# Reversing the column order of the gate, up and down products in a four-layer hybrid encoder

## The chip, the cores and the metric

The kernel runs on one core of a Trainium2 chip, as one program. The metric is the device time of one execution in microseconds. All tensors are float32 in memory; the large products use float32r operands, that is, float32 words that TensorE takes in one pass.

## What is computed

The reference is an encoder trunk on one sequence of 256 positions and 1024 channels, four layers deep. Each layer is a token mixer (in turn RWKV-7 time mixing, stick-breaking attention, sparse attention, RWKV-7 again) and then a feed-forward block:

```
x = x + mixer(rms_norm(x, norm_mix[i]))
x = x + swiglu(rms_norm(x, norm_ffn[i]), ffn_w_gu[i], ffn_w_down[i])

def swiglu(h, w_gu, w_down):
    g, u = jnp.split(h @ w_gu, 2, axis=-1)
    return (jax.nn.silu(g) * u) @ w_down
```

`w_gu` is 1024 x 5632 (gate and up, 2816 columns each) and `w_down` is 2816 x 1024, for each of four layers.

## The kernel before

**Layout.** Activations are kept transposed: a channel block of 128 is the partition dimension and the 256 positions lie along the free dimension. Every value that goes into a large product is kept as two float32r halves, a high one and a low one (the rest), side by side: `xg[:, c]` is one channel block with 2 x 256 columns, high half first. Weights arrive in pieces of 128 x 1024 floats and are split in the same way, by a cast on ScalarE (`wh`) and a subtraction on VectorE (`wl`); half of the gate and up pieces go to a buffer called `wring` instead.

**The gate, up and query/key products** come from `gemm1` (line 908). For each of 8 channel blocks it issues two matmuls into one PSUM bank. The first has the high weights as the stationary operand and the whole 512 columns of `xg[:, c]` (both halves) as the moving one, and writes all 512 columns of the bank. The second has the low weights and the 256 columns of the high half, and adds into the first 256 columns of the bank. The feed-forward block calls it 22 times for gate and 22 times for up in each of four layers; stick-breaking attention (layer 1) calls it 16 times more for `qk`. When a bank is complete, `add2` adds its two halves to each other, on ScalarE and VectorE.

**The down products** are the loop in `ffn` (line 1052): 8 output blocks in each layer, each the sum over 22 blocks of `h`, with the same two matmuls for each block and the same widths, into a bank called `dn`.

In this document *a pair* is such a 512-column matmul and the 256-column matmul behind it. There are 4 x 44 x 8 = 1408 pairs for gate and up, 4 x 8 x 22 = 704 for down, and 16 x 8 = 128 for `qk`: 2240 pairs, 4480 matmuls.

**Order.** Nothing is issued directly. Every operation is recorded (`Plan.record`, line 334), and a list scheduler with its own table of costs puts the operations of all engines in order before any is emitted (line 779 is the one line at which nearly all are emitted, so the profile shows L779 nearly everywhere and tiles tell the operations apart). A pair is one unit for the scheduler. Costs and dependences are taken from the number of elements and from the set of columns that a view touches, whatever their order.

**Other products.** The mixers have float32r products of their own (`po`, `rp`, `kp`, `vps`, `qi` and the `qk` of the sparse layer, in `gemm2`, `out_half` and `v_gemm`), plain float32 products (`qrot`, `qss`, `kss`, `vp`, ...) and many narrow ones. `warm_o` is a dummy bfloat16 product.

Of the kernel before, what the change touches and what calls it, by code (L numbers as in the profile page):

```python
# [23 lines left out]
S = 256  # L24
D = 1024
NC = D // P
NF = 11
# [268 lines left out]
class Plan:  # L296
# [15 lines left out]
    def unit(self, at_once=1, ns=0.0):  # L312

        plan = self

        class Unit:
            def __enter__(self):
                plan.unit_op = Op("tensor")
                plan.unit_op.ns = ns

            def __exit__(self, *_):
                op, plan.unit_op = plan.unit_op, None
                op.cost /= at_once
                op.cost = op.ns or op.cost
                plan._add(op)

        return Unit()
# [63 lines left out]
    def after(self, op, preds):  # L391
        op.preds |= set(preds)
# [390 lines left out]
def trunk(ctx: ExitStack, tc: tile.TileContext, xT_in, vecs_in, wts, lora_in, consts_in, id32_in, outT, order, layers=None):  # L783
# [7 lines left out]
    pe, dve, act, pool, sp = (plan.queue(n) for n in ("tensor", "vector", "scalar", "gpsimd", "sync"))  # L791
# [3 lines left out]
    def T(shape, group=None, name="t", dtype=F32):  # L795
        return plan.tile(sb, [P] + list(shape), dtype, group, name)
# [7 lines left out]
    def bank(name, group="ps"):  # L804
        return plan.tile(psum, [P, 512], F32, group, name, "psum")
# [48 lines left out]
    def f(ap):  # L854
        return ap.bitcast(F32)


    def piece(key, raw=None, parts=None):

        i = len(order)  # L860
        order.append(key)
        r = T([PIECE], "raw", f"raw{i}") if raw is None else raw
        sp.dma_start(r, wts[i])
        h, l = (T([PIECE], "wh", f"wh{i}", F32R), T([PIECE], "wl", f"wl{i}", F32R)) if parts is None else parts
        anye.copy(h, r)
        dve.tensor_tensor(l, r, f(h), op=ALU.subtract)
        return h, l
# [26 lines left out]
    def v3(t, n):  # L894
        return t.rearrange("p (k m) -> p k m", k=n)
# [4 lines left out]
    def flat(t):  # L900
        return t.rearrange("p a b -> p (a b)")

    def add2(t, o, eng=anye):

        eng.copy(t, o[:, S:])
        dve.tensor_tensor(t, o[:, :S], t, op=ALU.add)

    def gemm1(key, x, name, group="g", raw=None, parts=None):


        out = bank(name, group)
        wh, wl = [v3(t, NC) for t in piece(key, raw, parts)]
        for c in range(NC):
            with unit():
                pe.matmul(out, wh[:, c], flat(x[:, c]), start=(c == 0), stop=False)
                pe.matmul(out[:, :S], wl[:, c], x[:, c, 0], start=False, stop=(c == NC - 1))
        return out

    def gemm2(key, xs, name):
# [76 lines left out]
    def rstd_bcast(summed=False):  # L996
        if summed:
            ss = nstate["ss"]
        else:
            ss, sq = bank("ss"), t1("ssq")  # L1000
            anye.tensor_tensor(sq, nstate["acc"][:, 0], nstate["acc"][:, 1], op=ALU.add)
            exact(ss[:, :S], onesr, sq, [T([S], "t", "ssr", F32R) for _ in range(2)])
        return rsqrt_of(ss[:, :S], S, "rstd", 1.0 / D, eps_rms)
# [15 lines left out]
    def ffn(layer, after):  # L1019
        x = nstate["xg"]  # L1020
        rsb = None
        hs = [v.rearrange("p (i k a s) -> p i k a s", i=n, k=2, a=2)
              for v, n in ((T([4096], g, "h", F32R), 4) for g in ("SA", "SZ", "PR"))]

        ring = T([6, PIECE], "QC", "wring", F32R)

        def place(n):

            return {"parts": (ring[:, n // 2 % 3], ring[:, 3 + n // 2 % 3]) if n % 2 else None}

        for i in range(NF):
            gus = T([2, 2, S], f"s{6 + i % 2}", "gus")
            gs, us = gus[:, 0], gus[:, 1]
            since = len(plan.ops)
            for k in range(2):
                add2(gs[:, k], gemm1(("g", layer, 2 * i + k), x, "gate", **place(4 * i + k)), act if i >= 0 else anye)
            if i == 0:
                rsb = rstd_bcast()[:, None, :].to_broadcast([P, 2, S])
            dve.tensor_tensor(gs, gs, rsb, op=ALU.mult)
            act.activation(gs, gs, AF.Silu)  # L1040
            for k in range(2):
                add2(us[:, k], gemm1(("u", layer, 2 * i + k), x, "up", "ps", **place(4 * i + 2 + k)), act if i >= 0 else anye)
            if i >= 1:
                plan.in_turn(since, "gate", "up")
            dve.tensor_tensor(us, us, rsb, op=ALU.mult)
            dve.tensor_tensor(us, us, gs, op=ALU.mult)
            h = hs[i // 4][:, i % 4]
            act.copy(h[:, :, 0], us)
            dve.tensor_tensor(h[:, :, 1], us, f(h[:, :, 0]), op=ALU.subtract)

        n, since = 0, len(plan.ops)
        for m in range(NC):
            o = bank("dn", "g" if m % 2 else "ps")
            for k in range(2 * NF):
                if n % NC == 0:
                    wh, wl = [v3(t, NC) for t in piece(("d", layer, n // NC))]
                h = hs[k // 8][:, k // 2 % 4, k % 2]
                with unit():
                    pe.matmul(o, wh[:, n % NC], flat(h), start=(k == 0), stop=False)
                    pe.matmul(o[:, :S], wl[:, n % NC], h[:, 0], start=False, stop=(k == 2 * NF - 1))  # L1060
                n += 1
            for a in range(2):
                dve.tensor_tensor(xt[m // 2][:, m % 2], xt[m // 2][:, m % 2], o[:, a * S:(a + 1) * S], op=ALU.add)
            if m == NC - 1:
                plan.in_turn(since, "dn")
            if m % 2:
                after(m // 2)
# [500 lines left out]
    def stick(layer, after):  # L1568
# [12 lines left out]
        for p in range(8):  # L1581
            q, k = qk_[:, p, 0], qk_[:, p, 1]
            add2(q, gemm1(("sq", p), x, "qk"))
            add2(k, gemm1(("sk", p), x, "qk"))
            if p == 0:
# [377 lines left out]
```

## Time and profile before

| | |
|---|---|
| Median of 3 runs | 1396.13 us (1396.02 to 1396.16) |
| The profiled execution, its own time | 1397.01 us |
| Its span in the trace | 1395.1 us |
| TensorE (PE) busy | 1376.2 us, 99% of the span, 10404 matmuls |
| Weight loads (PEld) busy | 1184.4 us, 85% |
| VectorE (DVE) busy | 1076.0 us, 77% |
| ScalarE (ACT) busy | 802.8 us, 58% |
| HBM traffic | 217.14 MB read, 156 GB/s over the span |
| Granted TensorE clock | 1.00 throughout |

The profile is one execution. A row of its groups gives the engine, the operation, the tile written and the tiles read, the shape, the count, then the busy time and the mean duration in nanoseconds. Matmuls overlap each other, and their ends are modelled: the duration of one says more than the time it takes from its neighbours. What one matmul costs in a dense stretch is the distance from start to start, which the chain of waits gives as a total for a run of equal matmuls. The time of an execution is its span and a little around it, here 1.9 us.

### The profile page before, as it was taken

Reading aid. Unit: us, or ns where it says so; the run is one execution under the profiler, and the core shown is the slowest. Engines: PE = TensorE matmul, PEld = TensorE weight load, DVE = VectorE, ACT = ScalarE, POOL = GpSimd, SP = SyncE. Lnnn points to the kernel's source line nnn. Section 1 sums busy time; section 2 is a strip of 40 time slices with the busy share of each in tenths; the row PEclk is TensorE's granted clock in tenths of the full one; section 3 lists DMA queues with packets and bytes.
Section 4 is the critical chain, followed back from the end, with each engine's and each line's share of the span. In section 5 each row is a group of like instructions: output and inputs, shape, how many; then the busy total and the mean of one; then the engine's idle time right before and its main releaser. Section 6 shows DMA issues by size and latency. Waiting matters only on the chain.

```text
span 1395.1 us, 25701 instructions
## 1 busy us (share of the span) xinstructions
PE 1376.2 (99%) x10404; PEld 1184.4 (85%) x10404; DVE 1076.0 (77%) x1791; ACT 802.8 (58%) x1362; POOL 7.6 (1%) x16
## 2 busy tenths in 40 slices
PE   9999999999999999999999999999999999999998
PEld 6887888888888888888988788888878877888887
DVE  7998498876676788876668988876579985888754
ACT  3765576654456676554545876654438465766532
POOL 0000000000000000000000000000000000000000
PEclk9999999999999999999999999999999999999999
DMA  6423056665654357646654336766635220567654
GB/s 225 145 91 122 19 168 205 204 178 164 191 168 150 107 180 214 203 145 194 195 167 132 95 107 212 219 190 209 187 91 170 91 92 18 168 203 209 176 172 128
DMA packets 61317, 219.84 MB, mean 158 GB/s; under 512 B 6800, under 2 KB 8080, under 8 KB 60944
## 3 DMA queue, kind: packets, MB, share of 16 engines
q1 hardware_dynamic: 61200, 218.22, 50.8%
q8 instruction: 81, 1.33, 0.4%
q14 instruction: 36, 0.29, 0.1%
HBM read 217.14 MB, written 1.05 MB: 156 GB/s over the span
## 4 chain that ended last, share of the span: by engine, by line
PE 79%; DVE 12%; DMA 4%; ACT 3%; issue 2%; DVEq 0%; ACTq 0%
PE dn L779 17%; PE up L779 14%; PE gate L779 14%; PE qk L779 6%; DMA raw<-in_wts_dram 4%; PE rp L779 3%; PE kp L779 3%; PE po L779 3%; PE vps L779 3%; PE z L779 2%; DVE wl L779 2%; DVE inv L779 2%; DVE xtmp L779 1%; PE sc L779 1%; PE attn_o L779 1%
## 5 line engine op out<-in xcount | busy, mean ns | idle before, releaser
L779 DVE TENSOR_TENSOR wl<-raw,wh 128x1024 fp32r<-128x1024 f32 x285 | 347.9, 1223 | 142.0 <-ACT wh L779 140.2
L779 ACT CAST wh<-raw 128x1024 fp32r<-128x1024 f32 x268 | 280.8, 1049 | 234.0 <-PE dn L779 99.7
L779 PE MATMUL dn<-h,wh 128*128 128x512 f32 x704 | 244.2, 390 | 0.0
L779 PE MATMUL dn<-h,wl 128*128 128x256 f32 x704 | 198.5, 282 | 0.0
L779 PEld LDWEIGHTS dn<-h,wh 128*128 128x128 f32 x704 | 132.2, 188 | 27.7
L779 PE MATMUL gate<-xg,wring 128*128 128x512 f32 x704 | 133.0, 337 | 4.0 <-DVE wring L779 3.1
L779 PEld LDWEIGHTS dn<-h,wl 128*128 128x128 f32 x704 | 133.0, 189 | 0.0
L779 PE MATMUL up<-xg,wring 128*128 128x512 f32 x704 | 132.4, 336 | 0.0
L779 PEld LDWEIGHTS gate<-xg,wring 128*128 128x128 f32 x704 | 107.4, 188 | 22.0 <-DVE wring L779 5.4
L779 PE MATMUL gate<-xg,wh 128*128 128x512 f32 x352 | 125.5, 395 | 0.2
L779 PE MATMUL up<-xg,wh 128*128 128x512 f32 x352 | 125.1, 392 | 0.0
L779 DVE TENSOR_TENSOR wring<-raw,wring 128x1024 fp32r<-128x1024 f32 x88 | 107.4, 1221 | 17.3 <-ACT wring L779 16.4
L779 PEld LDWEIGHTS up<-xg,wring 128*128 128x128 f32 x704 | 107.4, 188 | 14.4
L779 ACT CAST wring<-raw 128x1024 fp32r<-128x1024 f32 x87 | 91.5, 1052 | 33.8 <-DMA raw<-in_wts_dram 25.8
L779 PE MATMUL up<-xg,wl 128*128 128x256 f32 x352 | 98.5, 280 | 0.0
L779 PE MATMUL gate<-xg,wl 128*128 128x256 f32 x352 | 98.4, 280 | 0.0
L779 PE MATMUL qk<-xg,wh 128*128 128x256 f32 (+1 forms) x384 | 96.7, 332 | 0.0
L779 PEld LDWEIGHTS gate<-xg,wh 128*128 128x128 f32 x352 | 66.0, 188 | 16.6 <-DVE xg L779 1.3
L779 PEld LDWEIGHTS up<-xg,wh 128*128 128x128 f32 x352 | 66.1, 188 | 14.5
L779 PEld LDWEIGHTS qk<-xg,wh 128*128 128x128 f32 x384 | 64.0, 188 | 9.7 <-issue 4.2
L779 PE MATMUL qk<-xg,wl 128*128 128x256 f32 x256 | 71.7, 280 | 0.0
L779 PEld LDWEIGHTS up<-xg,wl 128*128 128x128 f32 x352 | 66.1, 188 | 0.2
(306 smaller groups left out, 2592.9 us busy)
## 6 DMA issues: line engine op xcount, KB each, us to landing
raw<-in_wts_dram SPq DMA_DIRECT2D x397, 512.0 KB, 3.7
lora<-in_lora_dram SPq DMA_DIRECT2D x2, 1536.0 KB, 9.9
xt<-in_xT_dram SPq DMA_DIRECT2D x4, 256.0 KB, 3.7
lora<-in_lora_dram SPq DMA_DIRECT2D x2, 512.0 KB, 6.1
lg<-in_lora_dram SPq DMA_DIRECT2D x8, 128.0 KB, 3.9
inv<-in_id_dram SPq DMA_DIRECT2D x2, 512.0 KB, 3.7
out_dram<-xt SPq DMA_DIRECT2D x4, 256.0 KB, 3.6
lg<-in_lora_dram SPq DMA_DIRECT2D x2, 256.0 KB, 3.6
```

The source lines that it names most:

```text
L779: getattr(getattr(nc, o.eng), method)(*map(real, args), **{k: real(a) for k, a in kw.items()})
```

## The change

Both matmuls of a pair read their moving operand with a step of -1, from the last column to the first, and write their PSUM columns with a step of -1 too. Column 511 of the operand still ends up in column 511 of the bank; only the order in time within each matmul is turned round. The weights, the widths, the number of matmuls and the readers of the banks are as before.

```
--- before.py
+++ after.py
@@ -912,8 +912,8 @@
         wh, wl = [v3(t, NC) for t in piece(key, raw, parts)]
         for c in range(NC):
             with unit():
-                pe.matmul(out, wh[:, c], flat(x[:, c]), start=(c == 0), stop=False)
-                pe.matmul(out[:, :S], wl[:, c], x[:, c, 0], start=False, stop=(c == NC - 1))
+                pe.matmul(out[:, ::-1], wh[:, c], flat(x[:, c])[:, ::-1], start=(c == 0), stop=False)
+                pe.matmul(out[:, :S][:, ::-1], wl[:, c], x[:, c, 0][:, ::-1], start=False, stop=(c == NC - 1))
         return out
@@ -1056,8 +1056,8 @@
                     wh, wl = [v3(t, NC) for t in piece(("d", layer, n // NC))]
                 h = hs[k // 8][:, k // 2 % 4, k % 2]
                 with unit():
-                    pe.matmul(o, wh[:, n % NC], flat(h), start=(k == 0), stop=False)
-                    pe.matmul(o[:, :S], wl[:, n % NC], h[:, 0], start=False, stop=(k == 2 * NF - 1))
+                    pe.matmul(o[:, ::-1], wh[:, n % NC], flat(h)[:, ::-1], start=(k == 0), stop=False)
+                    pe.matmul(o[:, :S][:, ::-1], wl[:, n % NC], h[:, 0][:, ::-1], start=False, stop=(k == 2 * NF - 1))
                 n += 1
```

In the built program every engine has the same instructions in the same order as before. 4480 matmuls have other patterns (step -1 in place of 1, start at column 511 or 255 in place of 0). Beside that, 20 times the semaphore signal that stood on the 512-column matmul of a pair stands on the 256-column matmul right behind it, and 33 waits of TensorE on its own earlier matmuls name the later signal; one of these 33 was no such wait before.

## The prediction

> **What bounds the kernel now.** I read the page first, for the engine that is never free. The lines below are its span, the busy times, the granted clock, and the chain that ended last, by engine and then by tile.
>
> ```profile
> span 1395.1 us, 25701 instructions
> PE 1376.2 (99%) x10404; PEld 1184.4 (85%) x10404; DVE 1076.0 (77%) x1791; ACT 802.8 (58%) x1362; POOL 7.6 (1%) x16
> ...
> PEclk9999999999999999999999999999999999999999
> ...
> PE 79%; DVE 12%; DMA 4%; ACT 3%; issue 2%; DVEq 0%; ACTq 0%
> PE dn L779 17%; PE up L779 14%; PE gate L779 14%; PE qk L779 6%; DMA raw<-in_wts_dram 4%; PE rp L779 3%; PE kp L779 3%; PE po L779 3%; PE vps L779 3%; PE z L779 2%; DVE wl L779 2%; DVE inv L779 2%; DVE xtmp L779 1%; PE sc L779 1%; PE attn_o L779 1%
> ```
>
> TensorE is busy for 99% of the span at the full granted clock, and the chain lies on it for 79%. The tiles whose products change (`dn`, `up`, `gate`, and a part of `qk`) hold 17 + 14 + 14 + 6 = 51% of the chain, at most 711 us of 1395.1. So a change of pace in these products shows almost undiminished in the time.
>
> The second view is the chain of waits in order of time, in four dense stretches. A row is the start in us, the length in us, and what ran there: two runs of the feed-forward products, a run of `po`, and a run of `vps`.
>
> ```profile
> 280.04 5.55 PE up L779 x32
> 285.58 5.55 PE gate L779 x32
> ```
>
> ```profile
> 639.90 30.16 PE dn L779 x174
> ```
>
> ```profile
> 800.28 0.86 PE qrot L779 x2
> 801.14 2.81 PE po L779 x24
> ```
>
> ```profile
> 730.39 11.39 PE vps L779 x48
> ```
>
> 32 `up` matmuls are 16 pairs. They take 5.55 us, which is 347 ns a pair; a pair streams 512 + 256 = 768 columns, so a column costs 0.452 ns. The 174 `dn` matmuls, 87 pairs, take 30.16 us: again 347 ns a pair. `po` is 256 columns wide throughout: 2.81 us / 24 = 117 ns, 0.457 ns a column. `vps` is 512 wide: 11.39 / 48 = 237 ns, 0.463 ns a column. The price is thus by the column, whatever the width, and nothing fixed for each matmul is visible in these float32r products. No other engine interrupts these stretches: the chain stays on TensorE.
>
> Third, the list of who waited for whom, for TensorE alone. A row is the waiter, the releaser, the total in us, the number of times and the longest. This is its longest row:
>
> ```profile
> PE gate L779 <- DVE wring L779: 3.1, 7, 0.8
> ```
>
> All of TensorE's waits are of this size or smaller, and none of its rows names TensorE itself as the releaser. There is no wait here that the order of columns could remove.
>
> **The change part by part.**
>
> *Number of columns and matmuls: nothing.* The same 4480 matmuls (2240 pairs) stand in the same places of the same queue. The share they have is 2240 x 347 ns = 777 us. The groups of instructions by shape (count, then busy us, mean ns) confirm the widths for `dn`:
>
> ```profile
> L779 PE MATMUL dn<-h,wh 128*128 128x512 f32 x704 | 244.2, 390 | 0.0
> L779 PE MATMUL dn<-h,wl 128*128 128x256 f32 x704 | 198.5, 282 | 0.0
> ```
>
> *When a matmul can start and when its bank can be read: nothing.* A matmul waits for its whole operand before its first column, and `add2` and the additions to `xt` wait for the last matmul of a bank. Which column is last within it does not move these points.
>
> *Distance between two additions to one column: the same minimum.* In ascending order a column gets the pair's first addition, the second 512 columns later, and the next pair's first another 256 columns later. In descending order the gaps are 256 and then 512. The shortest is 256 columns in both cases (0.115 us at 0.452 ns), and `po`, which adds to the same 256 columns matmul after matmul, keeps its 0.457 ns a column with nothing but that gap. So I cost this at nothing; without that cover the surcharge would be visible in `po` already.
>
> *Moved signals: nothing.* 33 waits of TensorE for its own earlier matmuls now name the matmul behind the one they named. The tightest is the first `vps` of a run, which waits for a `qk` pair with 5 matmuls, 2048 columns, in between: 2048 x 0.452 ns = 0.93 us from the start after the awaited one to the waiter. A 256-column matmul starts 0.115 us ahead of its successor and lasts 0.28 us by the `dn` row above, so it is over some 0.75 us before it is needed. If that cover were gone, 33 times 0.28 us would be 9 us at most. Behind TensorE's waits stand only its own next matmuls, so nobody else is held.
>
> *The step of -1 in the moving read and in the PSUM write: the one unknown.* No matmul of the kernel before has a step other than 1 in either place, so no row here has its price. I bound it by neighbouring rows.
>
> - Below nothing: the fastest 256-column matmul of any kind in this trace is the bfloat16 dummy, 272 ns at least, against 282 ns for the 256-column `dn`. Were all 4480 matmuls to gain those 10 ns, the time would fall by 45 us. No reason for a gain appears in any row.
> - Nothing: the pace stays at 0.452 ns a column.
> - Above: the plain float32 products of this kernel stream 512 columns at about half pace. `qrot` above is two passes in 0.86 us, 0.43 us for 512 columns, 0.84 ns a column. At that pace a pair would take 768 x 0.84 = 645 ns, 298 ns more than now; times 2240 that is 668 us.
>
> ```profile
> L1797 PE MATMUL warm_o<-warm_x x140: 272/273/421, 1.2 to 1194.3; 128*128 128x256 bf16 x140
> ```
>
> I take nothing. The reversed operand has as many columns, as densely packed, as the `gate` rows do now, and the two distances in time that could matter (start of operand, reuse of a column) have just been shown not to. The nearest rows are the float32r rows themselves: `up`, `po` and `vps` differ in width, operand and bank, and lie within 0.452 to 0.463 ns.
>
> [...]
>
> *The sum.* The profiled execution took 1397.0 us (span 1395.1 and 1.9 around it); adding 0 leaves 1397.0. It lies 0.9 us above the median of the runs, 1396.13, so my forecast of the median is 1396.1 us.
>
> **The rivals.** A difference below about 0.2%, 2.8 us, could not be told from no change.
>
> *Rival 1, half pace (slower).* The stream moves two neighbouring columns at once when the addresses ascend and one when they don't, on the SBUF side or on the PSUM side. For it: TensorE does have a half pace in this very trace, 0.84 ns a column in `qrot`. Against it: `qrot`'s pace goes with plain float32 operands, not with an order. Price: 668 us if every pair lies on the path, so 1396 + 668 = 2064 us. The chain gives these tiles 711 of the 777 us they run, so at the least 711/777 of that, 611 us: 2007 us. It decides as soon as a column costs clearly more than 0.452 ns, since TensorE has no slack to hide it. [...]
>
> *Rival 2, a fixed price at the start of each matmul (slower).* Turning the walk round, or starting it at the far end, costs something once per matmul, and the columns then run at the old pace. The bound is the shortest distance between any two matmuls in the trace, in a run of 32-column ones:
>
> ```profile
> 131.25 0.62 PE cmb L779 x32
> ```
>
> 0.62 us / 32 = 19 ns from start to start, columns included, so what a start costs TensorE already is no more than that. One more such start for each of 4480 matmuls is 0 to 87 us: 1396 to 1483 us, 1440 in the middle. Against it: `po` at 117 ns and `vps` at 237 ns show no start price now.
>
> *Rival 3, faster.* An ordering effect of reads or writes that today's order suffers from, worth up to the 45 us above: 1351 us at best. Nothing in the profile points to it, except that it isn't excluded.
>
> *That the change does nothing at all*, because the two steps are turned back together somewhere below the built program, gives the forecast's time and can't be told from it by time.
>
> **How the numbers follow.** No change in time: 0.65, because all visible costs go by the column and none by position. Rival 1: 0.16. Rival 2: 0.15. Rival 3: 0.04. Faster is thus 0.04, the same 0.65, slower 0.16 + 0.15 = 0.31. The likeliest case has its own range of 1396.1 and 0.2% on each side, 1393.3 to 1398.9. To leave out no more than 2 in 10, the range has to take in rival 2 whole: 0.65 + 0.15 = 0.80, so 1393.3 to 1483. Rivals 1 and 3 stay outside.
>
> **What would show it right or wrong.** In the profile after, a run of 32 `up` or `gate` matmuls should again take 5.55 us in the chain, and 174 `dn` about 30.2 us, with `po` and `vps` as before. About 10 us for 32 `up` would be rival 1: both widths grow in proportion. Rival 2 would add the same number of nanoseconds to the 512- and to the 256-column matmul, up to 0.6 us to a run of 32. The list of waits should still have no row in which TensorE is released by TensorE; such a row at `vps`, `qi` or `dn` would say that the moved signals cost something after all. The forecast is wrong if the time leaves 1393.3 to 1398.9 for any reason.

## The result, and the profile after

| | before | changed |
|---|---|---|
| Median of 5 runs each | 1396.13 us | 1407.79 us |
| Profiled execution, time and span | 1397.01, 1395.1 us | 1405.01, 1403.2 us |
| Ratio of the runs, 95% interval | | 1.0079 (1.0063 to 1.0096) |

The changed kernel is slower, by 0.8%. In some executions of either kernel, e6, e11 and e13 below among them, the granted clock was 0.996 in place of 1.00 and the span longer (changed kernel: 1406.0 and 1408.7 us at 0.996, 1402.5 and 1403.2 at 1.00; kernel before, in the runs beside e1 to e4: 1398.3 to 1399.8 us at 0.996, 1393.5 to 1396.0 at 1.00), so the profiled spans at 1.00, 1395.1 and 1403.2 us, show the change better than the medians do: +8.1 us.

The page of the changed kernel, the same two lines as before:

```profile
span 1403.2 us, 25701 instructions
PE 1383.8 (99%) x10404; PEld 1183.1 (84%) x10404; DVE 1076.6 (77%) x1791; ACT 802.3 (57%) x1362; POOL 10.8 (1%) x16
```

TensorE's busy time has grown by 7.6 us; VectorE and ScalarE stayed within 0.6 us. The chain of waits of the changed kernel in the dense stretches (start, length, what ran):

```profile
280.37 5.62 PE up L779 x32
285.99 5.62 PE gate L779 x32
```

```profile
639.91 30.20 PE dn L779 x172
```

16 pairs take 5.62 us in place of 5.55, and 86 pairs of `dn` take 30.20 us: 351 ns a pair, where it was 347. The groups by shape show which of the two lasts longer (busy us, mean ns):

```profile
L779 PE MATMUL dn<-h,wh 128*128 128x512 f32 x704 | 247.4, 397 | 0.0
L779 PE MATMUL dn<-h,wl 128*128 128x256 f32 x704 | 198.5, 282 | 0.0
```

The 512-column matmul went from 390 to 397 ns, the 256-column one stayed at 282. The distances from start to start in the trace say the same. Here and below they are means over all pairs of a tile, without the few that include a wait (over 25 ns above the median). In `dn` the way from the 512-column matmul to the 256-column one grew from 228.4 to 233.0 ns, the way on to the next pair stayed (118.3 and 118.1): 346.7 against 351.1 ns. In `gate` and `up` it is 346.7 against 351.2 ns, in `qk` 346.7 against 351.1. Which interval grows doesn't say which matmul pays: in e4 below, where the 256-column matmul alone is turned, the way that leads up to it grows too, from 228.4 to 231.7 ns. TensorE's list of waits still has no row in which TensorE releases itself, and its longest row has become shorter:

```profile
PE gate L779 <- DVE wring L779: 2.3, 5, 0.8
```

**Where the 8.1 us lie.** 2240 pairs times 4.4 ns are 9.9 us. By the starts of the first `dn` and of what follows the last one, each of the four `dn` stages became 0.78 us longer (176 x 4.4 ns = 0.77). The stage with `qk` of stick-breaking attention became 0.54 us longer (128 x 4.4 = 0.56). The gate-and-up stages became 0.39, 1.71, 0.95 and 1.06 us longer, 4.1 in all where 4 x 352 x 4.4 = 6.2 us were to be expected. At the start of such a stage the chain stands on weights that are still being loaded and split. Its longest steps around the first `gate` matmuls are loads; here is one in the kernel before and then one in the changed kernel:

```profile
190.75 4.63 DMA raw<-in_wts_dram
```

```profile
195.11 3.54 DMA raw<-in_wts_dram
```

That a slower TensorE waits less for such weights fits the missing 2.1 us, and the row of `gate` above (2.3 us in place of 3.1); no run takes it apart. The remaining 0.4 us lie ahead of the first pair.

### The profile page after: what moved, and what is told of

It is laid out like the page before. It is cut to its first block, busy times and chain, and to the rows that moved or that the text cites. A ratio compares the mean times of both kernels' runs of the same rounds, so it can differ in the third digit from the quotient of the medians.

```text
span 1403.2 us, 25701 instructions
## 1 busy us (share of the span) xinstructions
PE 1383.8 (99%) x10404; PEld 1183.1 (84%) x10404; DVE 1076.6 (77%) x1791; ACT 802.3 (57%) x1362; POOL 10.8 (1%) x16
## 4 chain that ended last, share of the span: by engine, by line
PE 82%; DVE 9%; DMA 5%; ACT 3%; issue 1%; SPq 0%; DVEq 0%; ACTq 0%
PE dn L779 18%; PE up L779 15%; PE gate L779 14%; PE qk L779 6%; DMA raw<-in_wts_dram 5%; PE po L779 3%; PE rp L779 3%; PE kp L779 3%; PE vps L779 3%; PE z L779 2%; DVE wl L779 2%; PE vp L779 1%; PE sc L779 1%; DVE inv L779 1%; DVE xtmp L779 1%
## 5 line engine op out<-in xcount | busy, mean ns | idle before, releaser
L779 ACT CAST wh<-raw 128x1024 fp32r<-128x1024 f32 x268 | 280.6, 1048 | 238.3 <-PE dn L779 100.8
L779 PE MATMUL dn<-h,wh 128*128 128x512 f32 x704 | 247.4, 397 | 0.0
```

What stands on the lines that cost most here:

```text
L779: getattr(getattr(nc, o.eng), method)(*map(real, args), **{k: real(a) for k, a in kw.items()})
```

## The experiments

Theory A: the backward read of the moving operand costs. B: the backward PSUM write costs. C: the changed distance between two additions to one column costs. Later D: the moving read and the weight load get in each other's way in SBUF. E: a backward read costs by itself. F: the place of the moving operand by itself decides. Except where an interval is given, times are of single runs; the judgement rests on the pair times in the trace.

| kernel | `dn`, ns a pair | `gate` and `up`, ns a pair |
|---|---|---|
| before | 228.4 + 118.3 = 346.7 | 229.3 + 117.5 = 346.7 |
| changed | 233.0 + 118.1 = 351.1 | 234.2 + 117.0 = 351.2 |
| e1, read alone backward | 233.1 + 118.0 = 351.1 | 234.2 + 117.0 = 351.2 |
| e2, write alone backward | 228.3 + 118.3 = 346.7 | 229.3 + 117.5 = 346.7 |
| e3, 512-column matmul alone | 232.9 + 120.5 = 353.3 | 232.3 + 123.1 = 355.5 |
| e4, 256-column matmul alone | 231.7 + 115.0 = 346.7 | 233.7 + 116.4 = 350.0 |
| e5, changed, operands at 0 | 238.3 + 115.0 = 353.3 | 238.3 + 115.1 = 353.4 |
| e6, changed, operands at 64 | 235.8 + 117.5 = 353.3 | 233.9 + 117.3 = 351.2 |
| e7, changed, operands at 96 | 235.0 + 118.3 = 353.3 | 234.7 + 116.5 = 351.2 |
| e8, before, operands at 0 | 233.1 + 116.9 = 350.0 | 233.0 + 116.8 = 349.9 |
| e17, before, operands at 64 | 233.8 + 119.6 = 353.3 | 234.8 + 118.3 = 353.1 |
| e18, before, operands at 96 | 232.0 + 118.1 = 350.1 | 233.2 + 118.3 = 351.5 |
| e9, half the weights, forward | 230.0 + 117.5 = 347.5 | 230.8 + 116.3 = 347.1 |
| e10, half the weights, backward | 233.1 + 118.0 = 351.2 | 235.2 + 117.4 = 352.6 |
| e11, 16-byte groups down | 233.0 + 118.1 = 351.1 | 234.2 + 117.0 = 351.2 |
| e12, inside the groups down | 228.4 + 118.3 = 346.7 | 229.3 + 117.5 = 346.8 |
| e13, changed, all at 32 | 238.3 + 115.0 = 353.3 | 238.3 + 115.1 = 353.4 |
| e14, before, all at 32 | 231.5 + 116.8 = 348.3 | 232.0 + 116.8 = 348.8 |
| e15, 128-byte blocks down | 229.2 + 117.5 = 346.7 | 228.4 + 118.3 = 346.8 |
| e16, inside the blocks down | 234.2 + 116.9 = 351.1 | 233.3 + 118.1 = 351.3 |

**Read or write (e1, e2).** In both matmuls of `gemm1`, and the same in the `dn` loop:

```
# e1
pe.matmul(out, wh[:, c], flat(x[:, c])[:, ::-1], ...)
pe.matmul(out[:, :S], wl[:, c], x[:, c, 0][:, ::-1], ...)
# e2
pe.matmul(out[:, ::-1], wh[:, c], flat(x[:, c]), ...)
pe.matmul(out[:, :S][:, ::-1], wl[:, c], x[:, c, 0], ...)
```

> Only the moving operand of the pairs is read from the last column to the first; the PSUM columns are written in ascending order as before. (The gate, up, qk and down sums therefore come out with their positions reversed.) In the changed kernel the distance from the start of a 512-column matmul to the 256-column one behind it grew from 229 to 234 ns and the way back stayed at 118 ns, 4.4 ns a pair. Theory A, the backward read costs it: 234 and 118 ns here too, 32 up in 5.62 us, span about 1403, about 1405 us. Theory B, the backward PSUM write costs it: 229 and 118 ns, 5.55 us, 1396 us. Theory C, the smaller distance (256 in place of 512 columns) between the pair's two additions to one PSUM column costs it: additions are in the old order here, so 5.55 us, 1396 us. Both A and B in part: something between.

> Only the PSUM columns of the pairs are written from the last to the first; the moving operand is read in ascending order as before. (The sums again come out with their positions reversed.) Theory A, backward read: 229 and 118 ns, 32 up in 5.55 us, 1396 us. Theory B, backward write: 234 and 118 ns, 5.62 us, about 1405 us. Theory C, distance of the additions to one column: the order of the additions is that of the changed kernel, so 5.62 us, about 1405 us as well; the next two runs tell B from C.

e1 took 1406.02 us (ratio to the kernel before 1.0061, 1.0038 to 1.0084), e2 1398.63 us (1.0007, 0.9993 to 1.0022). The chain of e1, and then of e2:

```profile
285.65 5.62 PE gate L779 x32
```

```profile
290.04 5.55 PE up L779 x32
```

e1 has the pair time of the changed kernel to the tenth of a nanosecond, with the PSUM columns written forward; e2 has that of the kernel before, with PSUM written backward. Theory A stands; B falls, and with it C, since e2 adds to the columns in the changed kernel's order.

**Which matmul (e3, e4).** The four `::-1` of the change on the first matmul of the pair alone, or on the second alone:

```
# e3
pe.matmul(out[:, ::-1], wh[:, c], flat(x[:, c])[:, ::-1], ...)
pe.matmul(out[:, :S], wl[:, c], x[:, c, 0], ...)
# e4
pe.matmul(out, wh[:, c], flat(x[:, c]), ...)
pe.matmul(out[:, :S][:, ::-1], wl[:, c], x[:, c, 0][:, ::-1], ...)
```

> Only the 512-column matmul of each pair is turned round, read and write; the 256-column one runs in ascending order. Theories A and B with the cost on the 512-column matmul itself: 234 and 118 ns, 32 up in 5.62 us, about 1405 us. If the cost belongs to the turned 256-column matmul (its start comes later): 229 ns, 5.55 us, 1396 us. Theory C: the smallest distance between two additions to one column is now one column only, between the last column of the 512 and the first of the 256 behind it; if nearness costs, this must cost far more than 4.4 ns a pair, 10 ns or more, above 1418 us.

> Only the 256-column matmul of each pair is turned round, read and write; the 512-column one runs in ascending order. Theories A and B with the cost on the 512-column matmul: 229 and 118 ns, 32 up in 5.55 us, 1396 us. If the turned 256-column matmul delays its own start, 234 and 118 ns, 5.62 us, about 1405 us. If a turned matmul always pays some 5 ns but the weight load of the next one hides it behind 256 columns, again 5.55 us. Theory C: the smallest distance is between the 256's last column and the next 512's first, one column; if nearness costs, 10 ns or more a pair, above 1418 us.

e3 took 1411.65 us (1.0102, 1.0080 to 1.0124), e4 1401.61 us (1.0032, 1.0018 to 1.0046). Their chains, e3 first:

```profile
287.14 5.71 PE gate L779 x32
```

```profile
286.84 5.60 PE gate L779 x32
```

None of the expectations fits. Turning one matmul alone costs 6.6 to 8.8 ns a pair (the 512), or 0 in `dn` and 3.3 in `gate` and `up` (the 256), and turning both costs 4.4. The 3.3 is a mean: in e4 the pairs of `gate` and `up` take 347 and 353 ns by turns. So the costs don't add up by matmul, and the time of one depends on the direction of its neighbour. C falls once more: in e4 two additions to one column come a single column apart, and `dn` pays nothing for it. D was put forward next to explain this.

**The place in SBUF (e5 to e8, e17, e18).** `LEAD` sets where buffers start modulo 128 bytes. Before: operands `xg` and `h` at 32, weights `wh`, `wl` and `wring` at 0.

```
-LEAD = {"xb_0": 32, "wh_0": 0, "SZ_0": 32}
+LEAD = {"xb_0": 0, "wh_0": 0, "SZ_0": 0}     # e5 (changed kernel), e8 (kernel before)
+LEAD = {"xb_0": 64, "wh_0": 0, "SZ_0": 64}   # e6, e17
+LEAD = {"xb_0": 96, "wh_0": 0, "SZ_0": 96}   # e7, e18
```

> The changed kernel (backward read and write), with the buffers that hold the moving operands (xg, h) laid 32 bytes lower, at 0 modulo 128 bytes in place of 32, as the weight buffers are; work and order are the same. Settled by the runs so far: the extra 4.4 ns a pair come with the backward read alone, and which of the two intervals of a pair they fall on changes with which matmul is turned. Theory D, place: the moving read and the weight load of the next matmul, which runs beside it, get in each other's way in SBUF, and how often depends on the direction of the read and on where the two buffers lie to each other modulo 128 bytes; so the pair time changes here by 2 ns or more from 351 ns, in either direction, 32 up from 5.62 us by 0.03 us or more. Theory E, direction: a backward read costs some fixed nanoseconds wherever the operand lies: 351 ns a pair and 5.62 us again, about 1405 us.

> The changed kernel with the moving operands' buffers at 64 modulo 128 bytes. Theory D: the pair time differs from 351 ns, and from the kernel with them at 0, by 2 ns or more; with the right place it could be 347 ns or less again (32 up in 5.55 us or less, 1396 us or less). Theory E: 351 ns, 5.62 us, about 1405 us.

> The changed kernel with the moving operands' buffers at 96 modulo 128 bytes. Theory D: among the four places 0, 32, 64 and 96 the pair time spreads by 3 ns or more (32 up by 0.05 us or more). Theory E: 351 ns at all four, 5.62 us, about 1405 us.

> The kernel before (forward read and write) with the moving operands' buffers at 0 modulo 128 bytes. Theory D: the forward pair time of 347 ns belongs to the place 32; here it differs by 2 ns or more, more likely upward, to 349 or more (32 up in 5.58 us or more, 1400 us or more). Theory E: 347 ns a pair, 5.55 us, 1396 us.

> The kernel before with the moving operands' buffers at 64 modulo 128 bytes, weights at 0. Backward at this place the pair took 353 ns in dn and 351 in gate and up. If backward is the dearer direction at every place: 350 ns a pair or less here (32 up in 5.60 us or less). If only the place decides and directions mirror each other: 351 ns or more. A place that beats the kernel before would show 346 ns or less, 5.54 us, below 1395 us.

> The kernel before with the moving operands' buffers at 96 modulo 128 bytes, weights at 0. Backward at this place the pair took 353 ns in dn and 351 in gate and up. If backward is the dearer direction at every place: 350 ns or less here (32 up in 5.60 us or less). If only the place decides: 351 ns or more. A place that beats the kernel before would show 346 ns or less, below 1395 us.

Single runs gave 1409.99 (e5), 1409.21 (e6), 1411.21 (e7) and 1405.79 us (e8); e17 took 1407.59 us (1.0067, 1.0042 to 1.0092) and e18 1406.74 us (1.0056, 1.0032 to 1.0079). These totals also hold what `po`, `vps` and others gain or lose by the move: `vps`, 512 columns wide and always read forward, needs 227 ns with the operands at 0 and 233 at 32, and `po` 119.6 and 117.0. (In `vps` the moving operand is the weights, and `xg` is the stationary one.)

The place counts, for both directions, as D has it; E falls. Forward, the four places 0, 32, 64 and 96 cost on average 350, 347, 353 and 350 to 352 ns; backward 353, 351, and 353 in `dn` but 351 elsewhere at the last two. Not all of D's figures came: e6 was to differ from e5 by 2 ns and in `dn` both take 353.3, and the spread backward is 2.2 ns, not 3. That backward is always dearer is also wrong: at 64 both directions cost 353 in `dn`, and in `gate` and `up` backward is cheaper; e18 fits neither of its two expectations throughout. Of the four places, 32 is the best or as good as any in both directions, and none of the eight combinations beats the kernel before. The place modulo 128 bytes doesn't fix the pair time by itself, either: in e6 and e7 it is the same for all these tiles, and `dn` takes 353.3 ns where `gate` and `up` take 351.2.

**The length of the weight load (e9, e10).** All pairs of a sum but the first and the last use half of the weight columns; here `gemm1`, shortened (`m` stands for the expression in each index), in e10 with `[:, ::-1]` on both reads:

```
m = P if c in (0, NC - 1) else 64
pe.matmul(out[:m], wh[:, c, :m], flat(x[:, c]), ...)
pe.matmul(out[:m, :S], wl[:, c, :m], x[:, c, 0], ...)
```

> Forward read and write as before, but all pairs between the first and the last of a sum load only 64 of the 128 weight columns and write 64 partitions (the other half of the gate, up, qk and down sums is left out). It is the base for the next run: the distances inside a pair are read from the trace, the total time is not compared with before since the scheduler orders some units differently. Theory D, the moving read and the weight load running beside it get in each other's way: with half the weight load the 512-column matmul loses less, 229 ns falls to about 222 ns. Theory E, direction and place matter for the moving read alone: 229 ns stays.

> As the run before, with the pairs read and written from the last column to the first. Theory D: the extra of the backward read shrinks with the weight load, from 4.4 ns a pair to 2.2 ns or less. Theory E, a backward read costs by itself: 4.4 ns a pair or more remain (up to 9 ns, if the weight load had hidden the part of the 256-column matmul).

The weight loads of e9 (groups by shape; busy us, mean ns):

```profile
L779 PEld LDWEIGHTS dn<-h,wl 128*64 128x64 f32 x640 | 86.2, 135 | 0.0
```

The totals were 1429.89 us (e9) and 1440.07 us (e10). The loads last 135 ns in place of 189. The forward pair stays at 347 ns (347.5 in `dn`), and the backward read still adds 3.7 ns in `dn` and 5.5 in `gate` and `up`. D in the form of "the longer the weight load, the more is lost" falls. Other than its expectation says, e10 turned the reads alone and wrote PSUM forward, so that its sums have their positions reversed; by e2 no time hangs on that.

**Over which distance the order counts (e11, e12, e15, e16).** Only the reads change; `blk` splits the columns into blocks of `b` and turns the order of the blocks or that inside them:

```
def blk(t, b, down=False, inner=False):
    t = t.rearrange("p (a b) -> p a b", b=b)
    t = t[:, ::-1] if down else t
    return t[:, :, ::-1] if inner else t

pe.matmul(blk(out, 4), wh[:, c], blk(flat(x[:, c]), 4, down=True), ...)   # e11; e12: inner=True
                                                                          # e15, e16: 32 for 4
```

> Only the reads of the pairs change: groups of four columns (16 bytes) are taken from the last to the first, the four columns inside a group in ascending order; the PSUM columns are written ascending. (The positions inside the sums are mixed by this.) If it is the order in which the 16-byte groups are visited that costs, the pair takes 351 ns as in the changed kernel (32 up in 5.62 us), 1405 us; if it is the order inside a group, 347 ns (5.55 us), 1396 us. A pattern of two dimensions could cost something of its own; then both this run and the next lie above 351 ns.

> The counterpart of the run before: the groups of four columns are visited in ascending order, the four columns inside each from the last to the first; PSUM written ascending. (Positions inside the sums are mixed.) If the order of the groups costs: 347 ns, 5.55 us, 1396 us. If the order inside a group costs: 351 ns, 5.62 us, 1405 us.

> Only the reads of the pairs change: blocks of 32 columns (128 bytes) are taken from the last to the first, the columns inside a block in ascending order; PSUM is written ascending. (Positions inside the sums are mixed.) If the order of neighbouring 16-byte groups costs: nearly all neighbours ascend here, so 347 to 348 ns a pair, 5.55 us. If the far ends cost (a start at the far end, the jump from one matmul's last column to the next one's first): 351 ns, 5.62 us.

> The counterpart: blocks of 32 columns in ascending order, the columns inside each block from the last to the first; PSUM written ascending. (Positions inside the sums are mixed.) If the order of neighbouring 16-byte groups costs: 350 to 351 ns, 5.60 us or more. If the far ends cost: 347 ns, 5.55 us.

The chains of e11, e12, e15 and e16, in this order:

```profile
284.82 5.62 PE up L779 x32
```

```profile
282.46 5.55 PE up L779 x32
```

```profile
285.12 5.55 PE gate L779 x32
```

```profile
280.17 5.62 PE up L779 x32
```

Single runs gave 1409.74 (e11), 1399.65 (e12), 1396.87 (e15) and 1404.97 us (e16). The pair times fall cleanly on one side or the other. Groups of 16 bytes taken downward cost the full 4.4 ns (e11, 351.1 ns in `dn`); the four columns inside a group were reversed for nothing (e12, 346.7). Blocks of 128 bytes taken downward, ascending inside, cost nothing (e15, 346.7); ascending blocks with descending insides cost the full amount (e16, 351.1). So here it is the order of the 16-byte groups within 128 bytes. Whether the step that counts is 16, 32 or 64 bytes long is open: blocks between 16 and 128 bytes were not tried. The far ends and the jumps from matmul to matmul played no part (e15, 346.7), and a read pattern of two dimensions cost nothing by itself (e12 and e15, 346.7).

**Relative or own place (e13, e14).** The weights move to the operands' place:

```
+LEAD = {"xb_0": 32, "wh_0": 32, "SZ_0": 32}   # e13: changed kernel, e14: kernel before
```

> The changed kernel with the weight buffers moved by 32 bytes, so that weights and moving operands both lie at 32 modulo 128 bytes. In the run with the operands at 0 and the weights at 0 the backward pair took 238.3 + 115.0 ns, each nearly without spread; in the changed kernel (operands 32, weights 0) it takes 233 to 234 + 118 ns. Theory D, what counts is the place of the two relative to each other: 238.3 + 115.0 ns = 353.3 ns, 32 up in 5.65 us. Theory F, what counts is the place of the moving operand by itself: 233 to 234 + 118 ns = 351 ns, 5.62 us, as if the weights had not been moved.

> The kernel before with the weight buffers moved by 32 bytes, weights and moving operands both at 32 modulo 128 bytes. Forward with both at 0 the pair took 233 + 117 ns = 350 ns with a wide spread (230 to 241 for the first), forward with operands 32 and weights 0 it takes 229 + 118 ns = 347 ns. Theory D, relative place: 350 ns with the wide spread. Theory F, own place: 347 ns, 5.55 us.

The chain of e5 (all at 0) and of e13 (all at 32):

```profile
287.08 5.65 PE gate L779 x32
```

```profile
280.27 5.65 PE gate L779 x32
```

Single runs gave 1415.39 us (e13) and 1402.46 us (e14). e13 repeats e5 in both intervals, 238.3 + 115.0 ns, though its operands lie where the changed kernel has them. F falls: it is the place of the moving operand relative to the weights that counts. Two products that were never turned say the same: in e13 and e14 `vps` takes 227 ns and `po` 119.6, as in e5 and e8, and not the 233 and 117.0 of the kernel before. e14 agrees for the `dn` loop in one of four layers only, and shows something else. The chain of e8, the same direction and the same relative place, in the `dn` stages of the first and the third layer:

```profile
329.92 36.28 PE dn L779 x209
```

```profile
969.96 36.04 PE dn L779 x204
```

The first is 347.2 ns a pair by these rows, the second 353.3. By the distances in the trace the four layers of e8 take 346.7, 346.7, 353.3 and 353.4 ns, those of e14 346.7, 346.7, 353.4 and 346.7. The instructions, the direction and the places modulo 128 bytes are equal in all of them. The pace at this place has two levels. At the lower one every pair takes 346 or 347 ns; at the higher one pairs of 349, 350 and 361 ns follow each other in turn. The traces show where the level is set: where TensorE starts again after a wait. In the third layer of e8 the pairs take 347 ns up to a wait of `gate` for `wring` that ends at 859.7 us, and then the three lengths in turn until the last `dn`. In all eight layers of e8 and e14 the last pair that a wait stretches to 700 ns or more lies in the `gate` products; within five pairs of it one of the two levels is reached, and it holds for the 450 pairs that follow, to the end of the layer. What it is in the restart that decides was not tested. The forward `gate` and `up` at 96 (e18) have two levels as well: about 347 ns in the third layer and 353 in the others, there as 346 and 361 ns by turns.

## Why the prediction was wrong

- **What bounds the kernel: right.** TensorE had no slack (99% busy), and `dn` and `qk` passed on their whole surcharge (0.78 us for 0.77, 0.54 for 0.56). In the gate-and-up stages a third of it did not show, more than the chain share of 711 of 777 us had hinted; weights that arrive late are the likely reason.
- **Number, starts, additions, signals at nothing: right.** e2 shows that the order of the additions cost nothing (346.7 ns a pair); the list of waits has no row of TensorE on itself.
- **"The step of -1 in the moving read and in the PSUM write": this step failed.** I took nothing for it. For the write that is what was measured: 0.0 ns (e2). For the read it is 4.4 ns a pair (e1). I argued that "the two distances in time that could matter" had been shown not to, and never asked how the read walks through memory. I also used 0.452 to 0.463 ns a column as proof that width, operand and bank don't matter. The 0.463 was misread: the 11.39 us of `vps` include the longer steps at both ends of the run (335 and 319 ns), and between them a matmul takes 233.4 ns, 0.456 ns a column. Even so the spread is 1.2% (0.452 to 0.457), and the surcharge measured is 1.3% of a pair: rows that differ by as much as the effect can't exclude it. Part of the spread was of the same kind: within that run of the kernel before, `vps` matmuls of one shape take 238, 231 and 231 ns in turn, and 226 to 227 in e8, where `xg` lies at 0 modulo 128 bytes.
- **Rival 1, half pace: wrong.** 351 ns a pair against the 645 it would have given. The size is 1.3%.
- **Rival 2, a price at the start of each matmul: wrong in its mechanism.** The measured 1407.79 us lie inside 1393.3 to 1483 only because the range took in this rival, and that is luck: its band of 0 to 87 us was wide, and the 9.9 us of pair time came from something else. It should have added the same to both widths; in `dn` the way behind the wide one grew by 4.6 ns and the way behind the narrow one shrank by 0.2, and e15 has a start in the last block with no surcharge at all. Its bound of 19 ns was not the shortest distance in the trace either: some of the small `pS` matmuls start 2 ns apart.
- **Rival 3, faster:** no run beat the kernel before.

What is shown: the surcharge is a matter of the read, of the order of 16-byte groups within 128 bytes, and of where the operand lies relative to the weights. What is only argued: that the moving read and the weight load meet in SBUF. That moving the weights alone by 32 bytes takes the backward pair from 351.1 to 353.3 ns (e13) speaks for it; the half weight load speaks against any simple count of meetings (135 ns in place of 189, and the backward read still added 3.7 to 5.5 ns). How the start after a wait sets one of two levels stays open, and so does why `dn` and `gate` differ at equal places. Turning the direction of the weight load was not tried, nor places finer than 32 bytes.

## What to carry to other kernels

Where TensorE is the bound, the read order and the place of an operand can matter: here they were worth up to 9 ns a pair (355.5 in e3 against 346.7). Price such a change from the spread among like rows of the trace, and don't take that spread for noise; take distances inside a run, without the steps at its ends. Test a place for each read order: what a step of 32 bytes cost differed between them (from 32 to 64 in `dn`: 346.7 to 353.3 ns forward, 351.1 to 353.3 backward). Writing the PSUM columns backward was free (e2, 346.7 ns a pair).

## What had not been expected of the hardware

- With whole weights the mean pair time of a `dn` stage takes a few sharp values: 346.7, 350.0, 351.1 and 353.3 ns. In the kernel before, the changed kernel and e5 to e7 single pairs hardly differ from it (standard deviation below 1 ns). Elsewhere the same values are the mean of a short cycle of pairs: 349, 350 and 361 ns in the slow layers of e8, 349 and 351 in e18.
- The same pairs at the same places modulo 128 bytes can run a whole layer at 346.7 ns and the next at 353.3, and the level changes where TensorE restarts after a wait (e8, e14).
- Turning the 512-column matmul of a pair alone is dearer than turning both (e3 against the changed kernel: 353.3 to 355.5 against 351.1 ns).
- Halving the weight columns shortened the weight load from 189 to 135 ns and left the pair at 347 ns: the length of the load was not what spaced the matmuls.
